# Where layer 1's residual gates are multiplied: the projections' sums in PSUM on VectorE, or the weight tiles on GpSimd

## The chip, the cores and the metric

One program runs on one core of a Trainium2 chip. The metric is the device time of one execution in microseconds (us); the figure for a kernel is the median of its timed runs. The engines are named as the profile names them: PE is TensorE (PEld its weight loads), DVE is VectorE, ACT is ScalarE, POOL is GpSimd, SP is the engine whose queue issues every load and store of this kernel.

## The reference, cut to what matters

The model has two layers over 256 latent tokens and 256 context tokens of width 1024, all in 32-bit floats. The condition vector gives six rows per layer, two of which are gates. The latent stream of a layer, cut to what the change touches:

```python
sa, ca, ga, sf, cf, gf = _ada(c[:, None, :], w_ada[l], b_ada[l])
...
mix = _mix_out(o_a, o_b, o_c, diff_norm_w[l], lam_init, w_out[l])    # concat(heads) @ w_out, 1024x1024
x = _post_norm(x, ga * mix, ln1_g[l], ln1_b[l])                      # layernorm(ALPHA*x + ga*mix)*g + b
y = _conv_ffn(_modulate(x, sf, cf), w_up[l], conv_w[l], conv_b[l], w_down[l])   # ends in @ w_down, 2816x1024
x = _post_norm(x, gf * y, ln2_g[l], ln2_b[l])
```

A gate is one value for each of the 1024 output columns. Since `ga * (m @ W)` equals `m @ (W * ga)` with `ga` along the columns, it may be multiplied into the sums or into the weights. Layer 0 also updates the context stream, which has a gate of its own; layer 1, the last, has only the latent stream.

## The kernel before

Everything is held in 128-partition tiles. A matmul in full precision is made of three: each operand is split into a high part (rounded to the float32r type by a copy on ACT, L119) and the low rest (a subtraction on DVE, L120), and `mm3` (L132 to L134) adds hi*hi, hi*lo and lo*hi in PSUM.

`wsplit` loads a weight block of 128x1024 (512 KB) into a tile `raw` (a ring of four), may multiply it in place by a gate row on GpSimd (L115), and splits it into `whi` and `wlo` (rings of three). A block of `w_out` or `w_down` holds 256 rows of the weight (two groups `kk` of 128) by one half `hf` of 512 output columns. For one block and the two token tiles of layer 1 (t = 2, 3) PE does 2 x 2 x 3 = 12 matmuls of 512 columns.

The sums of a token tile t and a half hf lie in one bank of PSUM (three banks `acc` and one `ada` serve). When a sum is complete, `gated` adds it to the residual: in layer 0 a multiply by the gate row in place in PSUM (L876) and then `xr = ALPHA*xr + po` with a row sum (L877); in layer 1 only L877.

Layer 1's `w_out` (half 0 and 1, four blocks each) is worked in two parts. Three of the four row blocks come early, between the attention heads (`W3`, `W1` and `W0` in the written order `ORDERS[1]`, handled by `out_early`); the fourth comes in `token_major` with `allres`, token tile by token tile, each followed by its part of the layer norm (`head1`, `tail1`). Then the 22 pairs of `w_up` blocks run (`up_pair`), and then `token_major` for `w_down`: 11 blocks of half 0 for both token tiles, `gated` for both, seven blocks of half 1 for both, and the last four blocks of half 1 for t = 2 and then for t = 3, each followed by `gated` and `out_norm`, which writes the output.

`gate_row` loads a half of a gate (512 values, broadcast to all partitions, 256 KB) from DRAM into one of two tiles (slots 0 and 1, tags `bada` and `adarow`). In layer 1 before, both halves of a gate are loaded ahead of the first block that is multiplied by them.

GpSimd has other work as well: the relative-position bias of the neighbourhood heads (L725, L726: 128x256 tiles, in both layers), the power in each layer norm (L318) and the normalised tile `xn` (L340).

The order of the instructions on each engine is fixed when the kernel is built, by a planner that takes them by their place in the program, their estimated costs and the buffers that are free; each engine then runs its own list in order.

Of the kernel before, what the change touches and what calls it, by code (L numbers as in the profile page):

```python
# [11 lines left out]
ALU = mybir.AluOpType  # L12
# [60 lines left out]
def build(nc, tc, st, I, out):  # L73
    P = 128
# [12 lines left out]
    V, S, G, T = nc.vector, nc.scalar, nc.gpsimd, nc.tensor  # L87
# [4 lines left out]
    def acc():  # L92
        return bank("acc", 3)
# [10 lines left out]
    def load(dst, src):  # L104
        nc.sync.dma_start(out=dst, in_=src)

    def wraw(n):
        return wp.tile([P, n], F32, tag="raw", name="raw", bufs=4)

    def wsplit(src, n, pl=None, tag="", bufs=3, gate=None, ring=False):  # L110
        raw = pl.tile([P, n], F32, tag="raw" + tag, name="raw", bufs=1) if pl and bufs == 1 and not ring else wraw(n)
        load(raw, src)
        if gate is not None:
            r3 = raw.rearrange("p (k c) -> p k c", k=2)
            G.tensor_tensor(r3, r3, gate.unsqueeze(1).to_broadcast([P, 2, 512]), ALU.mult)  # L115
        pl = pl or wp
        hi = pl.tile([P, n], F32R, tag="whi" + tag, name="whi", bufs=bufs)
        lo = pl.tile([P, n], F32R, tag="wlo" + tag, name="wlo", bufs=bufs)
        S.copy(hi, raw)  # L119
        V.tensor_tensor(lo, raw, hi.bitcast(F32), ALU.subtract)  # L120
        return hi, lo
# [163 lines left out]
    def gate_row(l, r, cond, j, slot):  # L285
        t = tmp.tile([P, 512], F32, tag=("bada", "adarow")[slot], name="gate", bufs=1)
        load(t, garow[l, r][cond, 512 * j:512 * j + 512].partition_broadcast(P))
        return t
# [144 lines left out]
    def split_early(raw):  # L433
        hi = lp.tile([P, 1280], F32R, tag="ehi", name="ehi", bufs=2)
        lo = lp.tile([P, 1280], F32R, tag="elo", name="elo", bufs=2)
        split_from(raw, hi, lo)
        return kview((hi, lo), 2)
# [48 lines left out]
    for s in range(4):  # L486
        ks = (2 * s, 2 * s + 1)
        w = split_early(wes[s])
# [35 lines left out]
    for l in range(L):  # L524
        last = l == L - 1
# [7 lines left out]
        conds = [0] if last else [0, 1]  # L533
# [285 lines left out]
            pend.extend([ada(l, "b"), ada(l, "c")])  # L819
        outp = {}  # L820
        odone = []
        gts = []

        def out_mm(po, t, jb, w, kk, done):
            j = 2 * jb + kk
# [3 lines left out]
                not done and kk == 0, len(done) == 3 and kk == 1)  # L829

        def out_early(jb):
            if last and not gts:
                gts.extend(gate_row(l, "b", 0, hf, hf) for hf in range(2))
            for hf in range(2 if last else 1):
                w = wsplit(I["w_out"][l, hf, jb], 1024, gate=gts[hf] if last else None)
                for t in toks:
                    if not odone:
                        outp[t, hf] = acc() if len(outp) < 3 else adap()
                for kk in range(2):
                    for t in toks:  # L840
                        out_mm(outp[t, hf], t, jb, w, kk, odone)
            odone.append(jb)
# [27 lines left out]
        def gated(gates, po, t, hf):  # L870
            c = slice(512 * hf, 512 * hf + 512)
            if hf == 0:
                rsum[t] = sm.tile([P, 4], F32, tag="rsum", name="rsum")
                V.memset(rsum[t][:, 3:4], 0.0)
            if not last:
                V.tensor_tensor(po, po, gates[1 if t < 2 else 0], ALU.mult)  # L876
            V.scalar_tensor_tensor(xr[t][:, c], xr[t][:, c], ALPHA, po, ALU.mult, ALU.add,  # L877
                                   accum_out=rsum[t][:, hf:hf + 1])

# [34 lines left out]
        def token_major(pl, rnd, name, order, act, off, wpl, nres, head, tail, allres=False, nkeep=0):  # L914
            nb = len(order)

            def mm(po, t, jb, w, kk, first=None, fin=None):
                j = 2 * jb + kk
                first = jb == order[0] if first is None else first
                fin = jb == order[-1] if fin is None else fin  # L920
                tok = slice(128 * t - off, 128 * t - off + 128)
                c = slice(512 * kk, 512 * kk + 512)
                mm3(po, act(0, j)[:, tok], act(1, j)[:, tok], w[0][:, c], w[1][:, c],
                    first and kk == 0, fin and kk == 1)

            def blk(ws, hf, jb, n):
                if jb not in ws:
                    ws[jb] = wsplit(I[name][l, hf, jb], 1024, wpl, f"s{hf}", n, gts[hf] if last else None)
                return ws[jb]

            if allres:
                rem = [jb for jb in order if jb not in odone]
                ws = {}
                for i, jb in enumerate(rem):
                    for hf in range(2):
                        ws[jb, hf] = wsplit(I[name][l, hf, jb], 1024, wpl if i else None, f"r{hf}" if i else "", 1 if i else 3,
                                            gts[hf], True)
                for t in toks:
                    for i, jb in enumerate(rem):
                        for hf in range(2):  # L940
                            for kk in range(2):
                                out_mm(outp[t, hf], t, jb, ws[jb, hf], kk, odone + rem[:i])
                            if i == len(rem) - 1:
                                gated(None, outp[t, hf], t, hf)
                    head(t)
                tail(toks)
                return

            if last:
                gts[:] = [gate_row(l, rnd, 0, hf, hf) for hf in range(2)]  # L950
            gates = [None if last else gate_row(l, rnd, c, 0, c) for c in conds]
            if name == "w_out":
                pos = {t: outp[t, 0] for t in toks}
                rem = [jb for jb in order if jb not in odone]
            else:
                pos = {t: acc() if t else adap() for t in toks}
                rem = order
            passes = ([2, 3], [0, 1])[:len(conds)]
            st_ord = [order[:nb - nres] for _ in passes]
            if nkeep and len(passes) > 1:  # L960
                st_ord[1] = st_ord[0][-nkeep:] + st_ord[0][:-nkeep]
            blocks = [(0, jb) for jb in rem] + [(1, jb) for jb in st_ord[0]]
            if len(passes) > 1:
                blocks += [(1, jb) for jb in st_ord[1][nkeep:]]
            ready = []

            def fetch(n):
                while blocks and len(ready) < n:
                    hf, jb = blocks.pop(0)
                    ready.append(wsplit(I[name][l, hf, jb], 1024, gate=gts[hf] if last else None))  # L970

            def take():
                fetch(1)
                w = ready.pop(0)
                return w

            for i, jb in enumerate(rem):
                w = take()
                fetch(1)
                if i < len(rem) - 1:  # L980
                    pump(DP[0])
                for kk in range(2):
                    for t in toks:
                        mm(pos[t], t, jb, w, kk)
            for t in toks:
                gated(gates, pos[t], t, 0)
                if last:
                    first_half[t] = half_stats(xr[t], 0)
            gates = [None if last else gate_row(l, rnd, c, 1, c) for c in conds]
            ws = {}  # L990
            kept = {}
            for n, ts in enumerate(passes):
                pos = {t: acc() for t in ts}
                for i, jb in enumerate(st_ord[n]):
                    w = kept.pop(jb, None) or take()
                    if n == 0 and len(passes) > 1 and jb in st_ord[1][:nkeep]:
                        kept[jb] = w
                    elif not kept:
                        fetch(1)
                    pump(DP[1])  # L1000
                    for kk in range(2):
                        for t in ts:
                            mm(pos[t], t, jb, w, kk, i == 0, nres == 0 and i == nb - 1)
                for t in ts:
                    for jb in order[nb - nres:]:
                        w = blk(ws, 1, jb, nres)
                        for kk in range(2):
                            mm(pos[t], t, jb, w, kk, nres == nb and jb == order[0], jb == order[-1])
                    gated(gates, pos[t], t, 1)
                    head(t)  # L1010
                tail(ts)
# [246 lines left out]
```

## Time and profile before

| | before |
|---|---|
| timed runs | 1204.33 us median of 3 (1201.73 to 1211.84) |
| profiled execution | 1211.0 us, its span 1209.2 us |
| PE busy | 1131.6 us (94% of the span), 6704 matmuls |
| DVE busy | 876.0 us (72%) |
| ACT busy | 590.5 us (49%) |
| POOL busy | 170.3 us (14%), 134 instructions |
| TensorE clock, mean of the span | 0.971 of full speed |

The span runs from the first to the last instruction of the profiled execution; 1.8 us of that execution lie outside it. All positions below are us from the start of the span. Layer 1's attention ends at about 973, its up-projection runs from about 990 to 1123, and its down-projection from there to 1201.6.

### The profile page before, as it was taken

What the parts mean: (1) busy time and instruction counts of PE and PEld (TensorE: products, weight loads), DVE (VectorE), ACT (ScalarE), POOL (GpSimd) and SP (SyncE); (2) the same over time, 40 slices, a digit from 0 to 9 for tenths busy, and PEclk for the clock granted to TensorE, in tenths of its full rate; (3) what the DMA queues carried; (4) which work ended last, traced back from release to release, by engine and by line L of the source; (5) the groups of instructions that cost most, each with busy time, mean ns of one, the idle gap of its engine ahead of it and who ended that gap; (6) DMA issues with size and microseconds to landing.
All of it is one profiled execution on the core that took longest, in us unless ns stands there. A gap on an engine that the chain in (4) does not pass through costs nothing.

```text
span 1209.2 us, 17838 instructions
## 1 busy us (share of the span) xinstructions
PE 1131.6 (94%) x6704; PEld 912.8 (75%) x6704; DVE 876.0 (72%) x1497; ACT 590.5 (49%) x1063; POOL 170.3 (14%) x134
## 2 busy tenths in 40 slices
PE   5999999999989999999999999799999969999886
PEld 3766766686769888887877768787667659999664
DVE  4533777757688987969866787657766768888886
ACT  3235556656558534444432345555544455665321
POOL 0001000004022000000000011300024420003693
PEclk9999999999999999999999999999978879999988
DMA  9486312112334654635567875232112335555541
GB/s 364 169 288 238 122 36 70 36 40 84 108 109 135 202 157 137 199 122 179 157 239 271 279 263 175 81 122 74 36 53 79 118 102 161 188 178 167 182 145 64
DMA packets 58197, 179.18 MB, mean 148 GB/s; under 512 B 7016, under 2 KB 12408, under 8 KB 58112
## 3 DMA queue, kind: packets, MB, share of 16 engines
q1 hardware_dynamic: 58112, 178.05, 44.7%
q8 instruction: 53, 0.87, 0.3%
q14 instruction: 32, 0.26, 0.1%
HBM read 176.94 MB, written 1.08 MB: 147 GB/s over the span
## 4 chain that ended last, share of the span: by engine, by line
PE 73%; DVE 10%; DMA 6%; issue 4%; ACT 4%; POOL 3%; SPq 0%; DVEq 0%; ACTq 0%; POOLq 0%
PE acc L132 18%; PE acc L133 18%; PE acc L134 18%; PE sc L608 5%; DMA raw<-in_w_down 4%; PE tp L388 3%; DVE wlo L120 3%; PE tp L396 3%; ACT whi L119 2%; PE sc L813 2%; DMA raw<-in_w_ada 1%; POOL raw L115 1%; DVE adasc L210 1%; PE ada L231 1%; POOL xn L340 1%
## 5 line engine op out<-in xcount | busy, mean ns | idle before, releaser
L120 DVE TENSOR_TENSOR wlo<-raw,whi 128x1024 fp32r<-128x1024 f32 (+1 forms) x206 | 280.2, 1365 | 133.1 <-ACT whi L119 128.7
L119 ACT CAST whi<-raw 128x1024 fp32r<-128x1024 f32 (+1 forms) x206 | 212.6, 1037 | 270.7 <-PE acc L133 111.8
L132 PE MATMUL acc<-hhi,whi 128*128 128x256 f32 (+1 forms) x960 | 327.5, 342 | 6.6 <-ACT hhi L356 3.5
L133 PE MATMUL acc<-hlo,whi 128*128 128x256 f32 (+1 forms) x960 | 325.7, 340 | 0.5 <-DVE hlo L357 0.3
L134 PE MATMUL acc<-hhi,wlo 128*128 128x256 f32 (+1 forms) x960 | 324.8, 339 | 0.0
L132 PEld LDWEIGHTS acc<-hhi,whi 128*128 128x128 f32 x960 | 184.5, 192 | 31.7 <-issue 10.2
L133 PEld LDWEIGHTS acc<-hlo,whi 128*128 128x128 f32 x960 | 184.5, 192 | 22.4 <-issue 3.9
L134 PEld LDWEIGHTS acc<-hhi,wlo 128*128 128x128 f32 x960 | 184.3, 192 | 22.5 <-issue 4.6
L115 POOL TENSOR_TENSOR raw<-raw,gate 128x1024 f32<-128x1024 f32 x30 | 86.3, 2891 | 241.6 <-DMA raw<-in_w_down 134.8
L380 ACT ACTIVATE p<-sc,nm 128x512 f32<-128x512 f32 (+1 forms) x132 | 81.3, 618 | 33.7 <-DVE nm L377 32.1
L377 DVE TENSOR_REDUCE nm<-sc 128x1 f32<-128x512 f32 (+1 forms) x132 | 77.2, 597 | 22.7 <-PE sc L608 18.9
L608 PE MATMUL sc<-stk,stq 32*128 32x512 f32 (+3 forms) x324 | 78.4, 404 | 5.8 <-ACT p L380 5.8
L389 ACT COPY pT<-tp 128x512 f32<-128x512 f32 (+1 forms) x96 | 49.4, 515 | 63.4 <-PE tp L388 62.9
L318 POOL TENSOR_TENSOR rs<-mv,mhalf 128x1 f32<-128x1 f32 x20 | 14.7, 741 | 437.9 <-DVE mv L316 437.9
L608 PEld LDWEIGHTS sc<-stk,stq 32*128 32x128 f32 (+1 forms) x324 | 43.3, 189 | 32.0 <-ACT p L380 15.0
L132 PE MATMUL acc<-whi,gBhi 128*128 128x512 f32 x133 | 54.5, 411 | 7.3 <-DVE u L1048 4.2
L1044 ACT ACTIVATE u<-acc,conv 128x256 f32<-128x256 f32 (+1 forms) x94 | 60.7, 646 | 1.4 <-PE acc L134 1.3
L725 POOL TENSOR_TENSOR rpb<-rpb,m 128x256 f32<-128x256 f32 x24 | 19.9, 832 | 282.5 <-DVE p L656 175.3
L133 PE MATMUL acc<-wlo,gBhi 128*128 128x512 f32 x133 | 54.9, 413 | 4.4 <-DVE wlo L120 3.9
L1047 DVE SCALAR_TENSOR_TENSOR u<-acc,conv,u 128x255 f32<-128x255 f32 (+1 forms) x94 | 55.0, 585 | 5.3 <-ACT u L1044 5.3
L388 PE MATMUL tp<-ident,p 128*128 128x128 f32 x320 | 55.7, 291 | 2.4 <-DVE p L656 1.7
L210 DVE SCALAR_TENSOR_TENSOR ac<-raw,scT,ac 128x1024 f32<-128x1024 f32 x42 | 53.3, 1280 | 6.1 <-DMA raw<-in_w_ada 6.1
(266 smaller groups left out, 1956.2 us busy)
## 6 DMA issues: line engine op xcount, KB each, us to landing
raw<-in_w_up SPq DMA_DIRECT2D x94, 512.0 KB
raw<-in_w_ada SPq DMA_DIRECT2D x80, 512.0 KB
raw<-in_w_down SPq DMA_DIRECT2D x53, 512.0 KB
raw<-in_w_f SPq DMA_DIRECT2D x27, 512.0 KB
rawx<-in_w_ada_e SPq DMA_DIRECT2D x16, 512.0 KB
raw<-in_w_out SPq DMA_DIRECT2D x16, 512.0 KB
rpb<-in_rpb SPq DMA_DIRECT2D x24, 128.0 KB
gate<-scr SPq DMA_DIRECT2D x12, 256.0 KB
```

Of the source, the lines that this page charges most:

```text
L115: G.tensor_tensor(r3, r3, gate.unsqueeze(1).to_broadcast([P, 2, 512]), ALU.mult)
L119: S.copy(hi, raw)
L120: V.tensor_tensor(lo, raw, hi.bitcast(F32), ALU.subtract)
L132: T.matmul(o, lhsT=lh, rhs=rh, start=first, stop=False)
L133: T.matmul(o, lhsT=lh, rhs=rl, start=False, stop=False)
L134: return T.matmul(o, lhsT=ll, rhs=rh, start=False, stop=last).ins
L210: V.scalar_tensor_tensor(ac[c], raw, s, ac[c], ALU.mult, ALU.add)
L377: V.reduce_max(nm, sc[:, 0:nk], axis=AX.X, negate=True)
L380: hT["exp"] = S.activation(p[:, 0:nk], sc[:, 0:nk], AF.Exp, bias=nm, accum_out=sums[:, 0:1]).ins
L388: T.transpose(pt[:, 128 * kc:128 * kc + 128], p[:, 128 * kc:128 * kc + 128], ident)
L608: T.matmul(sc[:, 0:nk], lhsT=q[r, a, qs], rhs=k[r, b, 0:nk], start=t == 0, stop=t == 2, tile_position=(r.start, 0))
L1044: S.activation(t, po[:, c], AF.Identity, scale=cw[:, 1:2], bias=cw[:, 3:4])
```

## The change

`wsplit` loses its `gate` argument, and with it the multiply of 30 weight tiles on GpSimd (8 blocks of `w_out`, 22 of `w_down`). `gated` multiplies the sum by its gate row in both layers now, in place in PSUM on VectorE. The rows are loaded elsewhere: for `w_out` after the loads of the last blocks, for `w_down` half 0 ahead of the blocks and half 1 after the first half's `gated`, into slot 1.

```diff
-    def wsplit(src, n, pl=None, tag="", bufs=3, gate=None, ring=False):
+    def wsplit(src, n, pl=None, tag="", bufs=3, ring=False):
         raw = pl.tile([P, n], F32, tag="raw" + tag, name="raw", bufs=1) if pl and bufs == 1 and not ring else wraw(n)
         load(raw, src)
-        if gate is not None:
-            r3 = raw.rearrange("p (k c) -> p k c", k=2)
-            G.tensor_tensor(r3, r3, gate.unsqueeze(1).to_broadcast([P, 2, 512]), ALU.mult)
...
-        gts = []
...
         def out_early(jb):
-            if last and not gts:
-                gts.extend(gate_row(l, "b", 0, hf, hf) for hf in range(2))
             for hf in range(2 if last else 1):
-                w = wsplit(I["w_out"][l, hf, jb], 1024, gate=gts[hf] if last else None)
+                w = wsplit(I["w_out"][l, hf, jb], 1024)
...
-            if not last:
-                V.tensor_tensor(po, po, gates[1 if t < 2 else 0], ALU.mult)
+            V.tensor_tensor(po, po, gates[1 if t < 2 else 0], ALU.mult)
             V.scalar_tensor_tensor(xr[t][:, c], xr[t][:, c], ALPHA, po, ALU.mult, ALU.add,
                                    accum_out=rsum[t][:, hf:hf + 1])
...
                         ws[jb, hf] = wsplit(I[name][l, hf, jb], 1024, wpl if i else None, f"r{hf}" if i else "", 1 if i else 3,
-                                            gts[hf], True)
+                                            True)
+                gts = [gate_row(l, rnd, 0, hf, hf) for hf in range(2)]
                 for t in toks:
...
                             if i == len(rem) - 1:
-                                gated(None, outp[t, hf], t, hf)
+                                gated([gts[hf]], outp[t, hf], t, hf)
...
-            if last:
-                gts[:] = [gate_row(l, rnd, 0, hf, hf) for hf in range(2)]
-            gates = [None if last else gate_row(l, rnd, c, 0, c) for c in conds]
+            gates = [gate_row(l, rnd, c, 0, c) for c in conds]
...
-                    ready.append(wsplit(I[name][l, hf, jb], 1024, gate=gts[hf] if last else None))
+                    ready.append(wsplit(I[name][l, hf, jb], 1024))
...
-            gates = [None if last else gate_row(l, rnd, c, 1, c) for c in conds]
+            gates = [gate_row(l, rnd, c, 1, 1 if last else c) for c in conds]
```

## Rows read from the trace of the kernel before

**Rows 1.** The page, part 1: busy us, share of the span, instructions.

```profile
PE 1131.6 (94%) x6704; PEld 912.8 (75%) x6704; DVE 876.0 (72%) x1497; ACT 590.5 (49%) x1063; POOL 170.3 (14%) x134
```

**Rows 2.** Busy time by stretch, end: us, engines, granted clock, DMA share, GB/s.

```profile
1000.00:1109.00 109.00, 109.00 (x910) 109.00 (x910) 92.67 (x150) 68.42 (x113) 0.00 (x0) 1.00 0.58 179
...
1116.70:1119.80 3.10, 0.05 (x2) 0.05 (x1) 3.06 (x4) 0.07 (x1) 1.74 (x1) 1.00 0.50 169
...
1123.80:1128.00 4.20, 0.03 (x2) 0.04 (x1) 4.16 (x5) 1.87 (x4) 2.49 (x1) 1.00 0.42 125
1128.00:1132.20 4.20, 4.20 (x12) 3.29 (x13) 3.35 (x4) 1.20 (x2) 3.04 (x1) 0.59 0.32 125
1132.20:1160.30 28.10, 27.77 (x121) 22.18 (x119) 24.01 (x11) 10.00 (x11) 22.82 (x8) 1.00 0.55 187
1160.30:1163.40 3.10, 0.00 (x0) 0.00 (x0) 3.10 (x4) 1.04 (x1) 3.10 (x2) 0.88 0.54 169
1163.40:1169.40 6.00, 5.95 (x14) 4.68 (x15) 5.61 (x6) 1.04 (x1) 6.00 (x3) 0.50 0.25 87
...
1182.40:1186.00 3.60, 0.04 (x2) 0.01 (x1) 3.60 (x3) 1.31 (x2) 2.46 (x1) 1.00 0.44 146
1186.00:1190.20 4.20, 4.20 (x11) 3.30 (x12) 4.20 (x2) 0.86 (x1) 3.16 (x1) 0.59 0.00 0
```

**Rows 3.** VectorE's groups by shape, 1000 to 1109.

```profile
L120 DVE TENSOR_TENSOR wlo<-raw,whi 128x1024 fp32r<-128x1024 f32 x37 | 45.3, 1225 | 12.2 <-ACT whi L119 12.2
```

**Rows 4.** The same view, 1109 to 1190, and 860 to 960 (second row).

```profile
L120 DVE TENSOR_TENSOR wlo<-raw,whi 128x1024 fp32r<-128x1024 f32 x23 | 53.1, 2322 | 9.7 <-ACT whi L119 9.6
...
L120 DVE TENSOR_TENSOR wlo<-raw,whi 128x1024 fp32r<-128x1024 f32 x11 | 19.4, 1766 | 16.1 <-ACT whi L119 14.9 <-PE sc L608 1.1
```

**Rows 5.** GpSimd's groups by shape, 1109 to 1190.

```profile
L115 POOL TENSOR_TENSOR raw<-raw,gate 128x1024 f32<-128x1024 f32 x22 | 65.9, 3014 | 136.3 <-DMA raw<-in_w_down 134.8 <-DVE u L1048 1.4
```

**Rows 6.** Timeline of GpSimd, then of VectorE, near 1120: start, us, instruction.

```profile
1119.86 3.16 POOL L115 TENSOR_TENSOR raw<-raw,gate 128x1024 f32<-128x1024 f32 x1 [1.42 <-DVE u L1048]
...
1121.19 0.48 DVE L1048 SCALAR_TENSOR_TENSOR u<-acc,conv,u 128x255 f32<-128x255 f32 x1
1121.78 1.53 DVE L1053 TENSOR_TENSOR u<-u 128x256 f32<-128x256 f32 x1
```

**Rows 7.** Busy time by stretch, between attention heads; columns as in rows 2.

```profile
890.00:894.00 4.00, 2.36 (x15) 1.75 (x14) 3.97 (x4) 0.96 (x3) 4.00 (x2) 0.88 0.19 74
894.00:910.00 16.00, 15.86 (x50) 11.53 (x51) 10.05 (x23) 6.48 (x15) 0.63 (x1) 0.50 0.05 10
...
926.00:931.00 5.00, 3.57 (x14) 2.81 (x14) 4.15 (x7) 1.27 (x4) 4.93 (x6) 0.66 0.28 104
931.00:957.00 26.00, 23.35 (x154) 16.82 (x154) 20.34 (x30) 13.77 (x28) 15.34 (x13) 1.00 0.38 108
957.00:965.00 8.00, 7.95 (x23) 5.67 (x24) 5.16 (x12) 3.72 (x8) 1.47 (x2) 0.57 0.33 112
```

**Rows 8.** Layer 0, busy time by stretch: neighbourhood heads, then the down-projection.

```profile
280.00:300.00 20.00, 19.96 (x148) 14.30 (x148) 15.25 (x38) 13.01 (x36) 7.33 (x9) 1.00 0.17 54
...
680.00:700.00 20.00, 19.45 (x91) 14.96 (x90) 13.36 (x16) 6.57 (x7) 0.00 (x0) 1.00 0.87 288
```

**Rows 9.** Line 876, layer 0's gate: ns min/median/max, first and last start.

```profile
L876 DVE TENSOR_TENSOR acc<-acc,gate x14: 689/695/700, 328.0 to 745.7; 128x512 f32<-128x512 f32 x14
```

**Rows 10.** PE's waits from 645 to 745, layer 0's down-projection: us, times, longest.

```profile
PE acc L132 <- DVE xr L877: 1.9, 1, 1.9
```

**Rows 11.** Timeline of PE at layer 1's first layer norm.

```profile
983.90 1.97 PE L343 MATMUL tp<-ident,xn 128*128 128x128 f32 x8 [6.94 <-POOL xn L340]
```

**Rows 12.** Timeline of SP's queue: one of its last two loads of gate rows.

```profile
950.55 0.33 SPq L105 DMA_DIRECT2D gate<-scr  x1
```

**Rows 13.** The chain that ended last, in order of time.

```profile
1140.72 5.15 DMA raw<-in_w_down
...
1201.61 0.71 DVE xr L877 x2
```

More of the change, by code (lines that the diff above doesn't have):

```diff
@@ L927, in blk @@
                 if jb not in ws:
-                    ws[jb] = wsplit(I[name][l, hf, jb], 1024, wpl, f"s{hf}", n, gts[hf] if last else None)
+                    ws[jb] = wsplit(I[name][l, hf, jb], 1024, wpl, f"s{hf}", n)
                 return ws[jb]
```

## The prediction

> **What bounds the kernel now.** The page comes first: PE is busy for 94% of the span [rows 1], so little is to be had except where PE idles or runs slowly. The next view is therefore the busy time by stretch, with its column of the granted clock. In the up-projection of layer 1 (1000 to 1109) PE has no idle time, the clock is 1.00 (2.4 GHz) and GpSimd does nothing [rows 2]. In the down-projection that follows the reader sees four holes in PE of 3.05, 4.17, 3.10 and 3.56 us, with VectorE busy throughout and GpSimd too, and behind three of them stretches at 0.50 to 0.59, which are mostly 1.2 GHz [rows 2].
>
> VectorE is full there because its instructions have become longer. The subtraction that makes `wlo` takes 1225 ns each of 37 times while GpSimd rests [rows 3] and 2322 ns on average of 23 while GpSimd multiplies weight tiles; between the attention heads, 1766 ns [rows 4]. The 22 multiplies of `w_down` tiles take 3014 ns each [rows 5], and a subtraction that meets one waits for its end. The timeline shows this closely: one multiply runs from 1119.86 to 1123.02; the VectorE operation with one input in PSUM keeps its 0.48 us inside it, and the one after, whose two inputs both lie in SBUF, starts at 1121.78 and ends at 1123.3, with the multiply [rows 6]. So the multiplies on GpSimd cost PE time twice: they stand between a load and its split, and they hold up VectorE, which then frees PSUM banks late and hands `wlo` over late.
>
> **What the change removes, at the down-projection.** The holes add up to 3.05 + 4.17 + 3.10 + 3.56 = 13.9 us. The slow clock costs (1 - 0.59) x 4.2 twice and (1 - 0.50) x 6.0, together 6.4 us [rows 2]. All of it lies on the path, since PE has no slack from 990 to the end: 20.3 us. VectorE gets 23 x (2322 - 1225) ns = 25 us back in the subtractions alone, more than all the holes. What is late next? PE needs 12 matmuls per block: 27.77 us / 121 = 0.23 us each, so 2.75 us a block [rows 2]. ACT's copy and VectorE's 1.23 us subtraction are shorter. A load of 512 KB must then come every 2.75 us, 190 GB/s. The stretch before ran at 179 [rows 2] and layer 0's down-projection, which loads more, at 288 [rows 8]. So PE is the next limit, at full clock, and I take the whole 20.3. The lower end is in the rivals.
>
> **What it removes between the heads of layer 1** (eight `w_out` blocks). PE idles for 4.00 - 2.36 = 1.64 us at 890, 1.43 at 926 and 2.65 from 931 to 957. The clock is at its lower level (0.50) from 894 to 910, and partly from 926 to 931 and 957 to 965: 8.0, about 1.2 (0.34 of the 3.57 busy) and 3.4 us [rows 7]. Ends: nothing, if the bias tiles that GpSimd keeps hold VectorE up just as well, and the sum, 18.3 us. The nearest stretch without weight multiplies is layer 0's neighbourhood heads: GpSimd has 7.33 us of bias tiles in 20, PE is busy for 19.96 and the clock stays at 1.00 [rows 8]. That speaks for the upper half. But a stretch can't become shorter than VectorE's own work: 894 to 910 holds 10.05 us of it, so 6.0 of the 8.0 can come back, and 957 to 965 holds 5.16, so 2.8 of 3.4 [rows 7]. I take 1.64 + 6.0 + 2.8 = 10.4 us and leave the two holes after 926, where bias tiles run as well.
>
> **What it adds.** Eight multiplies of 128x512 in place in PSUM, 0.695 us each as layer 0's sixteen [rows 9], 5.6 us of VectorE in all, in three places:
> - The first layer norm of layer 1: four multiplies. PE already waits 6.94 us for `xn` here [rows 11], because VectorE, ACT and GpSimd work in turn; the sum of t = 2, half 0 is ready while PE still multiplies, so its multiply is hidden, the other three stand in front of the norm in VectorE's list: 0.7 to 2.1 us. I take 2.0, near the upper end, since VectorE has no free time there.
> - The change of halves in the down-projection: the second half of t = 3 needs a bank that `gated` frees, and `gated` is now two operations, with a subtraction perhaps ahead of it. In layer 0, where it has the multiply already, PE waits 1.9 us at this place [rows 10]. Bounds 0 and 3.1 (the hole that is there now [rows 2]); I take 1.9.
> - The end: the last sum, at 1201.61, is followed by VectorE's chain alone [rows 13], so one multiply lies on it in full: 0.7 us. That of t = 2 is covered by t = 3's last matmuls; without that cover it costs another 0.7.
>
> The moved loads of gate rows (four of 256 KB, as before) cost nothing. Each takes SP 0.33 us to issue, and the planner issued `w_down`'s at 950, long before their use [rows 12]. `w_out`'s now stand behind the last `w_out` loads, and `w_down`'s second behind the first half's; both tiles are free from the first norm on. If the first came late, `gated` would wait, and behind it on VectorE the whole norm: 2 to 3 us at most, by the time that a load takes. The waits that fall away on GpSimd free its list for the bias tiles and for the norm; the wait of `gated` for its row is the only one added.
>
> **Sum.** 20.3 + 10.4 - 2.0 - 1.9 - 0.7 = 26.1 us. The profiled execution took 1211.0, so it would take 1184.9. It lies 6.7 us above the median of the three runs, 1204.33; I take the same difference from the median: 1178. The ends of the terms give 20.3 + 18.3 - 0.7 - 0.7 = 37.2 (1167) and 20.3 + 0 - 2.1 - 3.1 - 1.4 = 13.7 (1191).
>
> **The rivals.**
> - *Only the down-projection gains.* The bias tiles of GpSimd still hold VectorE between the heads, and the softmax chains set the time there: 20.3 - 4.6 = 15.7 us, 1189. For it: the hole at 926 comes with bias tiles on GpSimd, too. Against it: layer 0's heads [rows 8].
> - *Loads pace the down-projection.* GpSimd itself mostly waited for `raw` [rows 5], and the chain has a load of 5.15 us on it [rows 13]. If loads stayed at the 169 GB/s that the holes show [rows 2], a block would take 524,288 B / 169 GB/s = 3.10 us, and 22 x (3.10 - 2.75) = 7.7 us would be lost: 18.4 us gained, 1186. Against it: 288 GB/s in layer 0, and that the ring of `raw` tiles was held by the multiplies.
> - *It doesn't do what it says.* The planner orders the whole second layer anew, and other holes, with their slow clock, come in place of these: 1204, within 1%.
> - *VectorE becomes the bound, slower.* If its subtractions are long for another reason than GpSimd, its work is what PE waits for, and 5.6 us more go on a full engine; at the two places where PE then waits for a bank (1.9 each) the clock falls as it did at 1163 (3.0 each): 5.6 + 2 x 4.9 = 15.4, 1220. It decides from the point at which a block costs VectorE more than PE's 2.75 us with GpSimd idle. Rows 3, at 1.23 us, are far from it.
>
> The Trainium skill speaks for this last one: Perfetto Trace Analysis, section Optimizing Scalar/DVE Operations, says that where VectorE is saturated, work may be given to ScalarE or even to GpSimd, and this change goes the other way; by that rule alone the time would be about 1210, the 5.6 us added to a full engine. The same paragraph warns that the two share a read port, so that moving work between them may not help; rows 4 and 6 are on the side of the warning.
>
> **How the numbers follow.** The forecast, 1178 with its terms' ends, 0.66; only the down-projection 0.14; loads 0.08; nothing 0.08; slower 0.04. About 1% (12 us; the three runs spread over 0.8%) is what a measurement of this kernel can tell from no change. Below 1192 lie the first three, 0.88, less 0.04 for their tails; within 1% the fourth and those tails, 0.12; above, 0.04. The range runs from 1166, below the best sum of the terms, to 1195, above the second and third case; it leaves out the fourth and fifth and some of the tails.
>
> **What would show it.** In the profile after: no L115, and eight more of L876 at 0.69 us; `wlo` at 1.23 us in the down-projection; no hole of 3 us in PE there except one of about 2 at the change of halves, and the clock at 1.00 up to the last matmul; some 60 us (22 x 2.75) from the first to the last matmul of `w_down`. Between the heads, no 16 us at 0.50. At the norm PE's wait grows from 6.9 to about 9 us. The prediction is wrong if `wlo` stays long with GpSimd idle, if PE's holes there now end on a load, or if the low clock comes back behind new, shorter holes: this last I know least about, since a hole of 1.43 us came before a fall at 926 [rows 7], and the holes that the change adds are about as long.

## The result, and the profile after

The changed kernel takes 1172.1 us, the median of four runs (1170.18 to 1174.29), beside 1208.09 us of the kernel before (1201.73 to 1214.4, four runs). The ratio is 0.9684, its 95% interval 0.9643 to 0.9724. The forecast was 1178 us in a range from 1166 to 1195. The profiled execution took 1174.29 us, its span 1172.5 us.

The page of the kernel after, parts 1 and 2: busy us of each engine, then the granted clock in 40 slices. It answers to [rows 1].

```profile
PE 1112.0 (95%) x6704; PEld 899.5 (77%) x6704; DVE 833.3 (71%) x1505; ACT 590.3 (50%) x1063; POOL 83.7 (7%) x104
...
PEclk9999999999999999999999999999999997999999
```

VectorE has eight more instructions than before and yet is busy for 42.7 us less (876.0 to 833.3). GpSimd has 30 instructions less. One slice of the clock is below 9, the one at the first norm of layer 1. (Numbers of lines have moved: L120 is L117 now, L876 is L869, L877 is L870.)

Where the 36.7 us of span (1209.2 to 1172.5) came back is read from busy times over whole stages. The heads are taken from the first `w_out` load to the last `w_out` matmul, the norm from there, the down-projection from its first matmul to its last. First the kernel before; columns: stretch, its length, busy us (and instructions) of PE, PEld, DVE, ACT and POOL, granted clock, DMA share, GB/s.

```profile
861.42:976.58 115.16, 108.14 (x635) 82.22 (x632) 78.54 (x139) 54.90 (x114) 35.55 (x26) 0.88 0.28 88
976.58:985.90 9.32, 2.36 (x10) 1.54 (x8) 6.53 (x17) 4.57 (x9) 4.94 (x7) 0.78 0.01 6
...
1122.73:1201.20 78.47, 67.25 (x266) 53.39 (x264) 63.80 (x44) 22.87 (x25) 54.69 (x20) 0.91 0.40 133
```

Then the same stages of the kernel after, and two stretches of 20 us. These answer to [rows 2, 7].

```profile
863.12:959.52 96.40, 96.05 (x636) 73.75 (x631) 66.91 (x140) 53.41 (x112) 15.08 (x18) 1.00 0.31 100
959.52:970.50 10.98, 2.35 (x10) 1.54 (x8) 8.15 (x21) 5.81 (x11) 4.94 (x7) 0.62 0.20 48
...
1103.71:1163.60 59.89, 59.89 (x265) 49.29 (x264) 35.17 (x44) 22.15 (x23) 0.98 (x1) 1.00 0.51 167
...
960.00:980.00 20.00, 9.07 (x41) 8.04 (x42) 15.41 (x34) 11.95 (x22) 6.17 (x8) 0.57 0.18 44
...
1120.00:1140.00 20.00, 20.00 (x90) 16.54 (x89) 12.04 (x15) 7.96 (x8) 0.00 (x0) 1.00 0.54 165
```

PE does the same matmuls (635 and 636 records in the heads). In the heads its idle time fell from 115.16 - 108.14 = 7.0 us to 0.35, and its busy time from 108.14 to 96.05 with the clock going from 0.88 to 1.00: 6.7 us of holes and 12.1 us of slow clock. In the down-projection the idle time fell from 11.2 us to none and the busy time by 7.4. GpSimd still does 15.08 us of bias tiles in the heads, and PE idles for no more than these 0.35 us.

VectorE's groups of instructions by shape, kernel after, 863 to 960 and 1100 to 1164 (busy us, mean ns, idle before); they answer to [rows 3, 4].

```profile
L117 DVE TENSOR_TENSOR wlo<-raw,whi 128x1024 fp32r<-128x1024 f32 x14 | 17.4, 1242 | 19.7 <-ACT whi L116 18.6 <-PE sc L605 1.1
...
L117 DVE TENSOR_TENSOR wlo<-raw,whi 128x1024 fp32r<-128x1024 f32 x22 | 26.8, 1224 | 20.8 <-ACT whi L116 20.8
```

The subtraction is back at its length without a neighbour in both places. All that PE waits for from 850 to the end, kernel after (line waited for, total us, times, longest), beside [rows 11]:

```profile
PE tp L340 <- POOL xn L337: 8.6, 1, 8.6
PE acc L129 <- ACT hhi L353: 1.6, 1, 1.6
PE tp L340 <- ACT hmod L348: 0.8, 1, 0.8
PE sc L605 <- ACT p L377: 0.2, 1, 0.2
```

No wait for a bank at the change of halves, none for a load, and one long one, the norm. What the change adds is seen in VectorE's timeline, kernel after: at the norm, at the change of halves, and at the end (start, us, instruction, idle before it).

```profile
956.09 0.70 DVE L869 TENSOR_TENSOR acc<-acc,gate 128x512 f32<-128x512 f32 x1 [0.76 <-PE acc L131]
...
961.38 0.69 DVE L869 TENSOR_TENSOR ada<-ada,gate 128x512 f32<-128x512 f32 x1
...
1133.48 1.29 DVE L869 TENSOR_TENSOR acc<-acc,gate 128x512 f32<-128x512 f32 x2
1134.68 0.68 DVE L870 SCALAR_TENSOR_TENSOR xr<-xr,acc 128x512 f32<-128x512 f32 x1
...
1164.04 0.70 DVE L869 TENSOR_TENSOR acc<-acc,gate 128x512 f32<-128x512 f32 x1 [0.26 <-PE acc L131]
1164.77 0.69 DVE L870 SCALAR_TENSOR_TENSOR xr<-xr,acc 128x512 f32<-128x512 f32 x1
```

Each multiply takes 0.70 us or less, as in [rows 9], and waits for a sum, never for its gate row. Stage by stage the span is made up so:

| stage | before | after | gained |
|---|---|---|---|
| up to the first `w_out` load | 861.4 | 863.1 | -1.7 |
| heads, to the last `w_out` matmul | 115.2 | 96.4 | 18.8 |
| norm, to the first matmul of `xn` | 7.3 | 9.0 | -1.7 |
| up-projection, to the first `w_down` matmul | 138.8 | 135.2 | 3.6 |
| down-projection, to the last matmul | 78.5 | 59.9 | 18.6 |
| behind the last matmul | 8.0 | 8.9 | -0.9 |
| sum | 1209.2 | 1172.5 | 36.7 |

The first row has the same instructions in both kernels; in the profiles of this study that load goes out at 859.6 to 865.0 us.

### The profile page after: what moved, and what is told of

It reads as the page before. It is cut to its first block, busy times and chain, and to the rows that moved or that the text cites. A ratio compares the mean times of both kernels' runs of the same rounds, so it can differ in the third digit from the quotient of the medians.

```text
span 1172.5 us, 17767 instructions
## 1 busy us (share of the span) xinstructions
PE 1112.0 (95%) x6704; PEld 899.5 (77%) x6704; DVE 833.3 (71%) x1505; ACT 590.3 (50%) x1063; POOL 83.7 (7%) x104
## 4 chain that ended last, share of the span: by engine, by line
PE 79%; DVE 7%; DMA 6%; ACT 3%; issue 3%; POOL 2%; SPq 1%; DVEq 0%; ACTq 0%; POOLq 0%
PE acc L129 20%; PE acc L130 20%; PE acc L131 20%; PE sc L605 6%; PE tp L385 3%; DMA raw<-in_w_down 3%; PE tp L393 3%; PE sc L810 2%; DVE adasc L207 1%; DVE wlo L117 1%; DMA raw<-in_w_ada 1%; ACT whi L116 1%; PE ada L228 1%; POOL xn L337 1%; DMA rawx<-in_w_ada_e 1%
## 5 line engine op out<-in xcount | busy, mean ns | idle before, releaser
L117 DVE TENSOR_TENSOR wlo<-raw,whi 128x1024 fp32r<-128x1024 f32 (+1 forms) x206 | 249.2, 1214 | 147.0 <-ACT whi L116 141.8
L605 PE MATMUL sc<-stk,stq 32*128 32x512 f32 (+3 forms) x324 | 75.0, 392 | 1.1 <-ACT p L377 0.9
L1036 ACT ACTIVATE u<-acc,conv 128x256 f32<-128x256 f32 (+1 forms) x94 | 60.8, 647 | 1.4 <-PE acc L131 1.3
L1039 DVE SCALAR_TENSOR_TENSOR u<-acc,conv,u 128x255 f32<-128x255 f32 (+1 forms) x94 | 54.9, 584 | 4.6 <-ACT u L1036 4.6
L1040 DVE SCALAR_TENSOR_TENSOR u<-acc,conv,u 128x255 f32<-128x255 f32 (+1 forms) x94 | 55.3, 588 | 2.3
L385 PE MATMUL tp<-ident,p 128*128 128x128 f32 x320 | 52.7, 279 | 0.1
L130 PE MATMUL acc<-wlo,gBhi 128*128 128x512 f32 x133 | 52.2, 393 | 0.5 <-DVE mv L313 0.5
L385 PEld LDWEIGHTS tp<-ident,p 128*128 128x128 f32 x320 | 36.7, 140 | 20.5 <-issue 8.6
L131 PE MATMUL acc<-whi,gBlo 128*128 128x512 f32 x133 | 51.8, 391 | 0.0
L129 PE MATMUL acc<-whi,gBhi 128*128 128x512 f32 x133 | 51.8, 392 | 0.0
```

What stands on the lines that cost most here:

```text
L129: T.matmul(o, lhsT=lh, rhs=rh, start=first, stop=False)
L130: T.matmul(o, lhsT=lh, rhs=rl, start=False, stop=False)
L131: return T.matmul(o, lhsT=ll, rhs=rh, start=False, stop=last).ins
L385: T.transpose(pt[:, 128 * kc:128 * kc + 128], p[:, 128 * kc:128 * kc + 128], ident)
L605: T.matmul(sc[:, 0:nk], lhsT=q[r, a, qs], rhs=k[r, b, 0:nk], start=t == 0, stop=t == 2, tile_position=(r.start, 0))
L1036: S.activation(t, po[:, c], AF.Identity, scale=cw[:, 1:2], bias=cw[:, 3:4])
```

## The experiments

The theory that the prediction rests on, exclusion: a GpSimd multiply that reads SBUF and a VectorE subtraction can't run side by side, so each multiply takes its own time from VectorE too. The rival, chain: the multiply is one more step of 2.4 to 3.5 us between a load and its split, so `whi` comes late. Both explain the result of the change; they differ when the multiply leaves the chain but stays on GpSimd. A third, from the prediction: VectorE is the engine that is short of time. Each kernel was timed beside the kernel before on its own chip; "heads" and "down" are the stages of the table above.

| kernel | median us | before there | ratio, 95% | heads | down |
|---|---|---|---|---|---|
| before | | | | 115.2 | 78.5 |
| after | 1172.1 | 1208.09 | 0.9684 (0.9643 to 0.9724) | 96.4 | 59.9 |
| multiply off the path | 1197.97 | 1209.22 | 0.9891 (0.984 to 0.9941) | 105.8 | 73.7 |
| weights on VectorE | 1173.5 | 1209.22 | 0.9699 (0.9641 to 0.9757) | 97.0 | 61.6 |
| delay in the path | 1172.74 | 1209.22 | 0.9691 (0.9641 to 0.9741) | 97.6 | 60.1 |
| down only | 1196.48 | 1209.22 | 0.9882 (0.9811 to 0.9952) | 118.1 | 59.9 |
| out only | 1189.04 | 1207.6 | 0.9819 (0.9761 to 0.9877) | 96.5 | 76.7 |
| write only | 1180.74 | 1207.6 | 0.9749 (0.97 to 0.9799) | 98.5 | 60.8 |
| read one | 1181.67 | 1210.44 | 0.9763 (0.9732 to 0.9794) | 99.9 | 65.1 |
| four pieces | 1202.8 | 1210.44 | 0.9935 (0.9903 to 0.9967) | 110.5 | 82.6 |
| no gate | 1172.38 | 1207.6 | 0.9688 (0.9639 to 0.9737) | 96.5 | 59.8 |
| weights out, sums down | 1173.3 | 1207.6 | 0.9698 (0.9642 to 0.9754) | 97.3 | 59.9 |

**The multiply off the path.** From the kernel before: GpSimd multiplies `raw` only after the subtraction has read it, so nobody needs the product (the added lines stand behind the split), and the gates multiply the sums in PSUM as in the kernel after.

```diff
         load(raw, src)
-        if gate is not None:
-            r3 = raw.rearrange("p (k c) -> p k c", k=2)
-            G.tensor_tensor(r3, r3, gate.unsqueeze(1).to_broadcast([P, 2, 512]), ALU.mult)
...
+        if gate is not None:
+            r3 = raw.rearrange("p (k c) -> p k c", k=2)
+            G.tensor_tensor(r3, r3, gate.unsqueeze(1).to_broadcast([P, 2, 512]), ALU.mult)
```

> The gates are multiplied on VectorE in PSUM as in the changed kernel, and GpSimd still does its 30 multiplies of 128x1024, but behind the subtraction, on the loaded tile that nobody reads any more: it is out of the chain from load to matmul. Theory A (a GpSimd multiply and a VectorE operation with two SBUF inputs exclude each other): per block of w_down 2.4 + 1.2 = 3.6 us of exclusive time against 2.75 us of matmuls, so the down-projection takes about 79 us again, subtractions of over 2 us, holes in PE and the slow clock come back; 1190 to 1212 us. Theory B (the multiply cost time because it stood between load and split): nothing of it is left, 1170 to 1180 us.

It gained 1.1% where the change gains 3.2%. The timeline of VectorE, then of GpSimd, in its down-projection:

```profile
1130.39 2.98 DVE L117 TENSOR_TENSOR wlo<-raw,whi 128x1024 fp32r<-128x1024 f32 x1 [0.36 <-ACT whi L116]
1133.70 3.00 DVE L117 TENSOR_TENSOR wlo<-raw,whi 128x1024 fp32r<-128x1024 f32 x1 [0.34 <-ACT whi L116]
1137.01 3.02 DVE L117 TENSOR_TENSOR wlo<-raw,whi 128x1024 fp32r<-128x1024 f32 x1 [0.31 <-ACT whi L116]
...
1122.35 28.91 POOL L120 TENSOR_TENSOR raw<-raw,gate 128x1024 f32<-128x1024 f32 x9 [1.22 <-DVE wlo L117]
```

The subtraction takes 3 us again, one every 3.31 us, and nine multiplies follow each other without a pause. PE needs a block every 2.75 us, so it starves, though no result of GpSimd is waited for by the matmuls. 22 blocks at 3.31 us are 72.8 us; the stage took 73.7. Exclusion stands, and the chain alone can't explain the loss: about two thirds of the gain is lost with the multiply out of the chain. What came back (in the profile 9.4 us in the heads, 4.8 in the down-projection) has to do with the multiply's place; which part of that is the chain was not separated.

There is another rival in this run. The multiply behind the subtraction keeps its `raw` tile longer, and the ring has only four, so the next load has to wait. SP's queue shows this, first here (1105 to 1185), then in "write only" further down (1100 to 1175), where three memsets a block, which read nothing, hold the tiles nearly as long (line waited for, total us, times, longest):

```profile
SPq L105 <- POOL raw L120: 57.3, 18, 5.0
...
SPq L105 <- POOL raw L120: 47.5, 18, 5.6
```

"Write only" has nearly the same wait for tiles, and its down-projection takes 60.8 us. So tiles that are kept longer are not enough to make the stage take 73.7.

**The weights on VectorE.** The kernel before with one letter changed.

```diff
-            G.tensor_tensor(r3, r3, gate.unsqueeze(1).to_broadcast([P, 2, 512]), ALU.mult)
+            V.tensor_tensor(r3, r3, gate.unsqueeze(1).to_broadcast([P, 2, 512]), ALU.mult)
```

> The kernel before with the 30 multiplies of weight tiles given to VectorE instead of GpSimd, at the same place in the chain; no multiply in PSUM in layer 1. Theory A: no GpSimd instruction is in the way; VectorE needs 2 x 1.23 = 2.46 us per block, under PE's 2.75, so the down-projection stays near 60 us, and between the heads some of the 8 x 1.23 = 10 us are not hidden; 1172 to 1185 us. Theory B: a multiply of 1.2 us stands in the chain in place of 3 us, so 40 per cent of the loss stays, about 1187. The rival of the prediction that VectorE is the bound: 37 us more on a full engine, 1205 or more.

VectorE's groups from 1095 to 1165, and its down-projection by stretch:

```profile
L120 DVE TENSOR_TENSOR wlo<-raw,whi 128x1024 fp32r<-128x1024 f32 x23 | 27.8, 1219 | 0.5 <-ACT whi L119 0.5
L115 DVE TENSOR_TENSOR raw<-raw,gate 128x1024 f32<-128x1024 f32 x20 | 24.3, 1222 | 2.9 <-DMA raw<-in_w_down 2.8
```

```profile
1100.00:1161.56 61.56, 60.10 (x266) 49.33 (x264) 55.03 (x61) 22.16 (x23) 0.98 (x1) 1.00 0.51 167
```

The same 30 multiplies, 30 x 1.22 = 37 us, now stand on the engine that seemed full, and still in the chain; the kernel gains what the change gains. VectorE was full because its subtractions were held, not because it had too much to do. Its work now fills 55.03 of 61.56 us there, and costs 1.7 us in that stage, which the missing multiplies at the norm and the end give back.

**A delay in the path.** The kernel after, with five multiplies of one column by one on GpSimd between each of the 30 loads and its split.

```diff
         load(raw, src)
+        for _ in range(5 if slow else 0):
+            G.tensor_tensor(raw[:, 0:1], raw[:, 0:1], onec, ALU.mult)
```

> The changed kernel, with five multiplies of one column (128x1, by one) on GpSimd, one behind the other, between the load and the split of each of the 30 blocks: a delay of some 2.5 to 4 us in the chain, as long as the multiply that was there, with hardly any use of SBUF. Theory A: 1172 to 1180 us, subtractions near 1.23 us. Theory B: the chain is as long as before, about 1205 us.

GpSimd's timeline shows the delay that each block gets:

```profile
1094.72 2.39 POOL L117 TENSOR_TENSOR raw<-raw,onec 128x1 f32<-128x1 f32 x5 [0.56 <-DMA raw<-in_w_down]
1097.63 2.33 POOL L117 TENSOR_TENSOR raw<-raw,onec 128x1 f32<-128x1 f32 x5 [0.53 <-DMA raw<-in_w_down]
```

The step came out shorter than was meant: 2.0 us a block on average in the down-projection, and 1.26 in some blocks, where the multiplies took 3.01. A step of that length in the same place costs nothing that can be measured, and the time is that of theory A. That the ring of four `raw` tiles hides it is argued, not shown. So a chain longer by some 2 us a block is no cause by itself; one longer by 3 us was not tried.

**One projection at a time.** "Down only" leaves `w_out`'s weights to GpSimd, "out only" leaves `w_down`'s.

The line that returns in each, in this order:

```diff
+                w = wsplit(I["w_out"][l, hf, jb], 1024, gate=gts[hf] if last else None)
...
+                    ready.append(wsplit(I[name][l, hf, jb], 1024, gate=gts[hf] if last else None))
```

> Only w_down's gate moves to VectorE; w_out's eight tiles are still multiplied on GpSimd. By the terms of the prediction 20.3 - 1.9 - 0.7 = 17.7 us are gained, 1190 against 1208. By the two traces, in which the holes at the end of the up-projection (3.6 us) and the down-projection (18.6) go and the end is 0.9 longer, 21 us, about 1187. If the falls of the clock between the heads also cost time later, less than 17.

> Only w_out's gate moves to VectorE; w_down's 22 tiles are still multiplied on GpSimd. By the terms of the prediction 10.4 - 2.0 = 8.4 us are gained, about 1200 against 1208. By the two traces (heads 18.8 shorter, norm 1.7 longer) 17 us, about 1191. If the two parts of the change simply add up, this gain and that of the run with w_down alone (13 to 14) give the whole, 36 to 37: then 23, about 1185.

The stages by stretch, first "down only":

```profile
861.20:979.25 118.05, 111.84 (x636) 84.35 (x632) 76.49 (x139) 55.11 (x114) 33.86 (x26) 0.86 0.28 86
1122.13:1182.03 59.90, 59.90 (x265) 49.32 (x264) 35.23 (x44) 22.11 (x23) 0.98 (x1) 1.00 0.52 167
```

and "out only":

```profile
1105.69:1182.39 76.70, 65.85 (x263) 52.35 (x264) 60.83 (x44) 22.96 (x25) 54.00 (x20) 0.93 0.43 139
```

Each stage is as after where GpSimd rests and as before where it multiplies. The two add up: 0.9882 x 0.9819 = 0.9703, beside 0.9684. In the table of stages, eight multiplies between the heads cost nearly as much (18.8 us) as 22 in the down-projection and just ahead of it (22.2). "Out only" gained 18.6 us by the medians, near what was expected; "down only" gained 12.7, less than the 17.7 and the 21 expected, and its heads are 2.9 us longer than before's. Its four runs lie 14.4 us apart (1188.95 to 1203.39), those of the kernel before 12.7, those of "out only" 5.1 and of the kernel after 4.1. That may point to GpSimd's multiplies between the heads, but "weights out, sums down" has none there and spreads over 9.3 us; with four runs each the cause stays open.

**GpSimd that only writes, and that reads one input.** As the first experiment, but in place of the multiply GpSimd does three memsets of the dead tile, or two copies of it onto itself.

```diff
+            for _ in range(3):
+                G.memset(raw, 0.0)
...
+            for _ in range(2):
+                G.tensor_copy(raw, raw)
```

> As the run with the multiplies behind the subtraction, but GpSimd fills the used tile with zeros three times instead of multiplying it: it is as busy, or nearly, and writes SBUF, but reads none of it. If what holds VectorE up is that GpSimd reads SBUF at the same time, the subtractions stay at 1.23 us and the time at 1170 to 1180 us. If any GpSimd instruction on SBUF holds it up, the subtractions grow to 2 us and more and the time to 1190 and more.

> As the run that fills the used tile with zeros, but GpSimd copies the used tile onto itself, twice per block: one input read, one output written, some 2.2 to 2.6 us per block. If any read of SBUF by GpSimd excludes VectorE's operations with two SBUF inputs, a block needs 2.2 + 1.2 = 3.4 us and more, the subtractions grow towards 2 us and the time is 1185 to 1200 us. If it takes two inputs on GpSimd, the subtractions stay at 1.23 us and the time at 1172 to 1181 us.

The groups of GpSimd (1105 to 1170) and of VectorE (1109 to 1170), and the down-projection, of "write only":

```profile
L120 POOL MEMSET raw<- 128x1024 f32 x66 | 61.0, 958 | 131.1 <-DVE wlo L117 129.4
...
L117 DVE TENSOR_TENSOR wlo<-raw,whi 128x1024 fp32r<-128x1024 f32 x20 | 24.5, 1224 | 24.6 <-ACT whi L116 24.6
...
1108.55:1169.37 60.82, 60.62 (x266) 49.06 (x264) 34.37 (x43) 22.15 (x23) 58.77 (x64) 1.00 0.53 173
```

and the same three of "read one" (both groups 1109 to 1170):

```profile
L120 POOL COPY raw<-raw 128x1024 f32<-128x1024 f32 x41 | 58.8, 1461 | 3.4 <-DVE wlo L117 2.3
...
L117 DVE TENSOR_TENSOR wlo<-raw,whi 128x1024 fp32r<-128x1024 f32 x19 | 29.1, 1540 | 20.9 <-ACT whi L116 20.8
...
1106.44:1171.50 65.06, 61.75 (x265) 48.92 (x264) 42.35 (x45) 22.23 (x23) 60.95 (x43) 1.00 0.52 161
```

GpSimd is busy nearly all the time in both. Memsets leave the subtraction at 1224 ns and the down-projection at 60.8 us. Copies stretch it to 1540 and are stretched themselves, to 1461 ns from 1037 for the shortest; the stage takes 65.1 us. So it isn't GpSimd's being busy, nor its writing, but its reading of SBUF that holds the subtraction up. The Trainium skill, SBUF — State Buffer, section "SBUF: two separate sides", describes this: GpSimd and VectorE share one pair of ports, held for a whole instruction, and a VectorE operation with two SBUF inputs needs it only against a GpSimd operation that reads SBUF. On which of GpSimd's operations hold the subtraction these two runs agree; the whole instruction comes out nearly, not exactly (last section).

The times don't separate the two runs: 1180.74 us is just above the range expected with reading as the cause, 1181.67 lies between the two forecasts for one input, and the ratios are 0.9749 and 0.9763. The difference is seen in the subtraction's length and in the down-projection alone.

The 6.6 us of span by which "write only" is behind the kernel after lie mostly elsewhere: 2.1 in the heads, 1.9 ahead of them. In the heads the trace shows an instruction of VectorE that memsets do hold up: the scaling of the softmax rows (L656), which reads one tile in SBUF, with one factor for each row, and writes it in place. Undisturbed it takes 0.48 us; in the one case that has memsets alone beside it, 1.18:

```profile
953.76 3.13 POOL L120 MEMSET raw<- 128x1024 f32 x3 [2.73 <-DVE wlo L117]
953.82 1.18 DVE L656 TENSOR_SCALAR p<-p,sums 128x512 f32<-128x512 f32 x1
```

So "only reading counts" holds for the subtraction, with its two tiles read, and not for every instruction of VectorE. How much of the 2.1 us comes from this is open.

**The multiply in four pieces.** The kernel before with each multiply cut into four of 128x256, so that VectorE may get in between.

```diff
-            r3 = raw.rearrange("p (k c) -> p k c", k=2)
-            G.tensor_tensor(r3, r3, gate.unsqueeze(1).to_broadcast([P, 2, 512]), ALU.mult)
+            for q in range(4):
+                r = raw[:, 256 * q:256 * q + 256]
+                G.tensor_tensor(r, r, gate[:, 256 * (q % 2):256 * (q % 2) + 256], ALU.mult)
```

> The kernel before with each multiply on GpSimd cut into four of 128x256. If what counts is the sum of the exclusive time, a block needs 4 x 0.73 (the bias tiles of that size) + 1.2 = 4.1 us in place of 3.6, and the down-projection about 91 us in place of 79: 1215 to 1225 us. If what counts is how long one hold keeps VectorE, a subtraction waits for 0.7 us at most in place of 2.4: below 2 us each, and 1185 to 1198 us.

VectorE's and GpSimd's groups from 1109 to 1190:

```profile
L121 DVE TENSOR_TENSOR wlo<-raw,whi 128x1024 fp32r<-128x1024 f32 x22 | 31.0, 1413 | 40.6 <-ACT whi L120 40.6
...
L116 POOL TENSOR_TENSOR raw<-raw,gate 128x256 f32<-128x256 f32 x83 | 80.2, 1007 | 0.0
```

The subtraction falls to 1413 ns, so it does get in between two pieces; but GpSimd now has no idle time at all: 83 pieces fill 80.2 us, 3.87 us for the four of a block, and the down-projection takes 82.6. The heads gain 4.7 us. Neither the cure nor the harm that was expected came: 1202.8 us lies between the two forecasts. ScalarE's copies now wait for GpSimd's pieces (1109 to 1197: line waited for, total us, times, longest):

```profile
ACT whi L120 <- POOL raw L116: 52.4, 19, 5.5
```

So the stage is paced by GpSimd, whose piece takes 1007 ns on average and 717 at the shortest. That in a full stretch the sum of both engines' work counts, and not the length of one hold, fits this and is argued, not shown.

**The price of the gates in PSUM.** The kernel after without layer 1's eight multiplies, which leaves the gate out.

```diff
-            V.tensor_tensor(po, po, gates[1 if t < 2 else 0], ALU.mult)
+            if not last:
+                V.tensor_tensor(po, po, gates[1 if t < 2 else 0], ALU.mult)
```

> The changed kernel without any gate in layer 1 (left out: the eight multiplies of the sums by their gate rows; the rows are still loaded). It gives the price of the eight multiplies. By the prediction's terms 2.0 + 1.9 + 0.7 = 4.6 us, about 1168. By the traces 1.7 at the norm and 0.7 to 0.9 at the end, 2.5 us, about 1170. If all were hidden, 1172.

PE's timeline at the first norm:

```profile
967.39 1.97 PE L340 MATMUL tp<-ident,xn 128*128 128x128 f32 x8 [6.95 <-POOL xn L337]
```

PE's wait there is 6.95 us without the multiplies, as in [rows 11], and 8.60 with them; the end is 8.1 us and 8.9. Together they cost 2.1 to 2.5 us of span, too little for the medians to show (1172.38 and 1172.1).

**A mixture.** `w_out`'s weights are multiplied on VectorE, so the norm is spared, and `w_down`'s sums in PSUM.

Against the kernel after:

```diff
+        if gate is not None:
+            r3 = raw.rearrange("p (k c) -> p k c", k=2)
+            V.tensor_tensor(r3, r3, gate.unsqueeze(1).to_broadcast([P, 2, 512]), ALU.mult)
...
-                w = wsplit(I["w_out"][l, hf, jb], 1024)
+                w = wsplit(I["w_out"][l, hf, jb], 1024, gate=gts[hf] if last else None)
...
-            V.tensor_tensor(po, po, gates[1 if t < 2 else 0], ALU.mult)
+            if gates:
+                V.tensor_tensor(po, po, gates[1 if t < 2 else 0], ALU.mult)
```

> A mixture: w_out's eight tiles are multiplied on VectorE ahead of their split, w_down's sums in PSUM. From the run with all weights on VectorE the norm keeps PE's wait of 6.9 us in place of 8.6 and the heads are 0.6 us longer; from the changed kernel the down-projection keeps its 60 us. 1 us less than the changed kernel, about 1171; at most 2, which this measurement hardly shows. If VectorE's eight multiplies between the heads meet the bias tiles on GpSimd, 1173 to 1176.

Its norm wait is 6.94 us, its heads are 0.9 us longer, and the time, 1173.3, is that of the kernel after within the scatter. No version beat it.

## Why the prediction was right, and where its sizes were off

The mechanism was as forecast, and the time lies 6 us below the forecast, inside the range. Its sum on the profiled executions was 26.1 us of gain; 36.7 came. By the medians the gain is 36.0 us, 9.9 more than forecast; that the time itself is off by only 6 is in part luck, since the forecast stood on 1204.33, the median of three runs, and a fourth moved that to 1208.09.

The prediction let a multiply cost time in two ways: as a step between a load and its split, and by holding VectorE up. The runs bear out the second. They don't show the first: a delay of some 2 us a block in its place cost nothing measurable. Step by step:

- *The down-projection, 20.3 us.* Right: 18.6 in the stage and 3.6 ahead of it (the first of the four holes lies before the first `w_down` matmul) make 22.2. PE went to 59.9 us, forecast "some 60", without a hole and at clock 1.00.
- *The heads, 10.4 us.* Mis-sized: 18.8. The listed holes and slow stretches added up to 18.3, the upper end, and nearly all of that came back (6.7 of holes, 12.1 of slow clock). Two steps failed. The smaller, 2.6 us, is "a stretch can't become shorter than VectorE's own work". The 10.05 us that VectorE did while PE crawled from 894 to 910 need not stay in that stretch; they can run next to other matmuls. Such a floor holds only for the stage as a whole, and there it is far away: 66.91 us of VectorE in 96.40. The larger, 5.3 us, is leaving out what lies from 926 to 957 (holes of 1.43 and 2.65 us, 1.2 of slow clock) because bias tiles run there as well. They run there still, 15.08 us of GpSimd in all, and PE idles for 0.35 us in the whole stage; "down only" shows that the eight multiplies were the cause. The trace of before has it already. The hole of 1.43 us ends on the softmax scaling, which was held up by a weight multiply and not by a bias tile (kernel before: GpSimd, VectorE, PE):

```profile
924.77 2.36 POOL L115 TENSOR_TENSOR raw<-raw,gate 128x1024 f32<-128x1024 f32 x1 [10.09 <-DMA raw<-in_w_out]
924.81 3.47 DVE L656 TENSOR_SCALAR p<-p,sums 128x512 f32<-128x512 f32 x2
...
927.56 1.09 PE L388 MATMUL tp<-ident,p 128*128 128x128 f32 x4 [1.43 <-DVE p L656]
```

- *The norm, -2.0.* Right: -1.7, by PE's wait of 8.60 after 6.94.
- *The change of halves, -1.9.* Mis-sized: nothing. The multiplies and additions run from 1133.48 to 1135.9, and PE is busy for 20.00 of the 20.00 us around them. The row of layer 0 [rows 10] was no measure for it; that its four token tiles, where layer 1 has two, are the reason is argued, not shown.
- *The end, -0.7.* Right: -0.9.
- *Moved loads, nothing.* Right: no `gated` waited for its row.

The terms miss by 8.4 in the heads, 1.9 at the change of halves, 1.9 in the down-projection, 0.3 at the norm, less 0.2 at the end and 1.7 ahead of the heads: 10.6 us, the difference of 36.7 and 26.1. Of it 6 are seen in the medians, since the profiled execution after lies 2.2 us above its median where that of before was taken as 6.7 above.

The rivals: *only the down-projection gains* falls with the heads' 18.8 us. *Loads pace the down-projection* falls with PE's 59.89 of 59.89 us; the mean of 167 GB/s there is lower than the 190 that the blocks need, because the first of them had landed before. *It doesn't do what it says* falls with the result. *VectorE becomes the bound* falls in "weights on VectorE", which puts 37 us there and not 5.6. The rule of the Trainium skill cited for it (Perfetto Trace Analysis, Optimizing Scalar/DVE Operations) pointed the wrong way here, and its warning of the shared port the right one.

What the prediction said that it knew least, the low clock behind new holes, didn't come: between 880 and the last matmul the one stretch below 1.00 begins at the norm (0.57 from 960 to 980), and it was there before (0.50 from 985 to 995). The one hole that grew is the wait at the norm, by 1.7 us. What makes the clock fall was not tried.

## What to carry to other kernels

An engine that is idle in the profile is not free: before work goes to GpSimd, look at what VectorE does at the same time, and if GpSimd's instruction reads SBUF while VectorE's reads two tiles of it, count its time on both. Look at VectorE's other instructions too: the softmax scaling here, with one tile read, was held up as well. The sign in a trace is not a wait but an instruction that is longer than its group's usual time; compare the mean of one shape in stretches with the other engine busy and idle. And a floor by one engine's work holds for a stage as a whole, not for a slow window cut out of it.

## What the runs showed of the hardware that was not expected

- An in-place copy on GpSimd, with one input, holds VectorE's subtraction up as well, if less: 1540 ns in place of 1225. Memsets don't: 1224 ns with GpSimd busy for 61.0 us.
- A memset on GpSimd does hold up an in-place scaling on VectorE with one tile read: 1.18 us in place of 0.48, seen once.
- With the multiply off the path, a multiply (2.34 us at its shortest in that run) and a subtraction (1.23) alternate every 3.31 us, 0.26 less than their sum. So the exclusion isn't quite whole by the recorded lengths, of which those on GpSimd are rough.
- 37 us of multiplies in SBUF moved from GpSimd to VectorE gain 3% of this kernel; each takes 1.22 us there, and 2.36 at the shortest on GpSimd.
